# Query units of a hybrid decoder trunk: one copy out of PSUM by ScalarE, all later readers on the copy

## The chip, the core and the metric

The kernel runs on one core of one Trainium2 chip. The metric is device time in microseconds, the median of three runs. Every time below comes from the runs, from the profile of one further execution, or from answers of its trace.

The core's engines are named as follows: PE is TensorE (matmuls; PEld its weight loads), DVE is VectorE, ACT is ScalarE, POOL is GpSimd, SP issues DMAs.

## What is computed

A trunk of two residual layers over 2048 tokens of width 1024, in float32. Each layer normalises its input, projects it, runs three branches with SiLU gates and projects back:

```python
for layer in range(DEPTH):                       # DEPTH = 2
    xn = rms_norm(h, norm_g[layer])
    if layer % 2 == 0:
        u, v, ga, xb, gb, qm, gm = _split(xn @ w_in_even[i], EVEN_SIZES)
        ya = chunked_sgu(u, v, ...) * silu(ga)
        yb = multiscale_pool(xb, b_w[i], b_scale[i]) * silu(gb)
        ym = memory_attention(qm, mem_n, ...) * silu(gm)
    else:
        qc, kc, vc, gc, da, db, gd, qm, gm = _split(xn @ w_in_odd[i], ODD_SIZES)
        yc = swa_sink_attention(qc, kc, vc, ...) * silu(gc)   # 8 heads, window 128
        yd = conformer_conv(da, db, ...) * silu(gd)           # 31 taps
        ym = memory_attention(qm, mem_n, ...) * silu(gm)      # 4 heads, 256 memory rows
    h = h + concatenate([ya_or_yc, yb_or_yd, ym]) @ w_out[i]
```

Both attentions normalise their queries by head (64 wide): `q * rsqrt(mean(q*q) + eps)`.

## The kernel before

**Tiles.** The tokens are cut into four blocks of 512. One block through one layer is a stage; there are four even and four odd stages, run in the order even 0, even 1, odd 0, even 2, odd 1, even 3, odd 2, odd 3. The odd stages begin near 475, 960, 1430 and 1685 us.

**Wide units.** A projection is made in units of 128 output channels by 512 tokens (`proj`): 8 chunks, each three matmuls 128x512 (`mm3`, L126 to L128), since every operand is split into a rounded high half and a low half that holds what the rounding left. So a unit is 24 wide matmuls into one PSUM bank "mm".

**Query units.** `query_steps` makes 32 of them: two memory-query units in each stage, and four window-query units in each odd stage. In a unit, after `proj`:

- `stack_queries` casts each half of the partitions to the high half (ScalarE, L315, 64x512, twice) and subtracts it from the projection to get the low half (VectorE, L123, 64x512, twice). The two halves go to different partitions, so that one score matmul multiplies high and low together.
- ScalarE squares the projection (L363). Four small matmuls (L366, with as many weight loads) sum the squares by head into the bank "pv". VectorE adds a constant (L369, tile qss), GpSimd raises to the power -1/2 (L370).

All five of the first readers read the PSUM bank. The scores (L320, L321) take the query halves as weights and the keys km or kt as moving data.

**PSUM.** Eight banks: two "mm", one "cv", four "tr" (scores and transposes take turns there), one "pv". The sums of squares, the window values (L873), the memory values (L426) and one even-stage product share the one "pv" bank.

**An odd stage.** Its order is a string of steps: f fills (a wide unit of the background list, four query units, gates), S0 to S3 are the window scores of four token tiles, V0 to V3 their values, s0 to s3 and v0 to v3 the same for the memory, g and d the conv's units. The relevant part is "S3 V2 f4 s0 V3 e d2 s1": the fill of four wide units (two memory-query units, then two gates) ahead of s0 and V3. This place is called the tail of the fill phase below; "the last wide unit" is the second gate of that fill.

- A window score step S: 16 score matmuls, copies by ScalarE, masks and maxima by VectorE, eight exponentials with sums by ScalarE (L845), a normalisation by GpSimd (L852).
- A value step V (`swa_values`): eight transposes (L860) into two "tr" banks; of each bank ScalarE copies (L863) and VectorE multiplies by a mask (L864) the four heads' weights, and GpSimd masks ScalarE's copy (L866); eight value matmuls 128x512 (L873); four products by VectorE (L881).
- A gate: one wide unit, tanh by ScalarE (L349), a product by VectorE (L351).
- The depthwise conv is 31 taps on VectorE (L698, 128x512), put between the other VectorE work wherever the scheduler finds room. Memory maxima on VectorE are L407.

**What sets the order.** The source is written in steps; the framework's list scheduler then orders each engine's instructions by a simulated timeline. So the order on every engine is fixed at build time and depends on the durations and dependencies that the scheduler models. An edit in one place can move instructions in others.

Of the kernel before, what the change touches and what calls it, by code (L numbers as in the profile page):

```python
# [12 lines left out]
AF = mybir.ActivationFunctionType  # L13
# [8 lines left out]
TB = 512  # L22
# [30 lines left out]
def trunk(ctx: ExitStack, tc: tile.TileContext, x, mem, par, par1, wkv, w_v, w_cm0, w_kvc, w_cm1, w_o0, w_o1, awt, bw, dpw, abse, out):  # L53
    nc = tc.nc
    V, A, G, T = nc.vector, nc.scalar, nc.gpsimd, nc.tensor
# [26 lines left out]
    def pv_bank():  # L82
        return bank("pv", 1)

    def short(dt=F32):
        return pp_.tile([P, TB + 14], dt, tag="u2", name="u2", bufs=4)

    def half(tag, bufs, dt=F32):
        pool = mov if tag in ("yh", "yl", "q") else sb
        return pool.tile([P, TB], dt, tag=tag, name=tag, bufs=bufs)  # L90

    def small(tag, n):
        return sm.tile([P, n], F32, tag=f"s{n}", name=tag, bufs={1: 6, 2: 6, 4: 8, 6: 2, 8: 10, 16: 4, 32: 2}[n])
# [4 lines left out]
    def par_of(name):  # L98
        t, a, b = _COLS[name]
        return (pc, once)[t][:, a:b]  # L100
# [21 lines left out]
    def lo_of(eng, lo, raw, hi):  # L122
        eng.tensor_tensor(lo, raw, hi.bitcast(F32), op=ALU.subtract)  # L123
# [188 lines left out]
    def stack_queries(pb):  # L312
        qq = [half("q", 8, F32R) for _ in range(2)]
        for g, (rows, other) in enumerate(((lowr, high), (high, lowr))):
            A.copy(qq[g][rows], pb[rows])  # L315
            lo_of(V, qq[g][other], pb[rows], qq[g][rows])
        return qq

    def score(out, q, g, cols, keys):
# [10 lines left out]
    def proj(xn, w_cm, unit, after=None):  # L330
        wh, wl = view(wslot(w_cm[unit], key=("cm", int(w_cm is w_cm1), unit)), "p (k c) -> p k c", k=KC)
        pb = mm_bank()
        for k in range(KC):
            with tc.issue_after(after.ins) if after and k == 0 else ExitStack():
                mm3(pb, wh[:, k, :], wl[:, k, :], xn[0][:, k, :], xn[1][:, k, :], k == 0, k == KC - 1)
        pump(2)
        return pb
# [16 lines left out]
    def query_steps(st, w_cm, units, heads, tag):  # L354
        qs = []
        n_u = len(units)
        r = small(tag, NT * heads).rearrange("p (t h) -> p t h", t=NT)

        def step(n, u):
            pb = proj(st["xn"], w_cm, u)  # L360
            qs.append(stack_queries(pb))
            sq = short()
            A.activation(sq[:, :TB], pb, AF.Square)  # L363
            sp = pv_bank()[:, :2 * NT]
            for tt in range(NT):
                T.matmul(sp[:, 2 * tt:2 * tt + 2], lhsT=sq[:, tt * P:(tt + 1) * P], rhs=par_of("bones"),  # L366
                         start=True, stop=True)
            t = small("qss", 2 * NT)
            V.tensor_scalar(t, sp, 64 * EPS, None, op0=ALU.add)  # L369
            G.tensor_tensor(r[:, :, n:n + n_u + 1:n_u], t.rearrange("p (t g) -> p t g", t=NT),  # L370
                            nhalf[:, :2 * NT].rearrange("p (t g) -> p t g", t=NT), op=ALU.pow)

        return (qs, r), [lambda n=n, u=u: step(n, u) for n, u in enumerate(units)]
# [683 lines left out]
```

## Time and profile before

| | us |
|---|---|
| median of three runs | 1932.83 (1929.33 to 1933.11) |
| profiled execution | 1935.3 |
| its span, first to last instruction | 1933.6 |
| TensorE busy | 1893.0 (98%) |
| VectorE busy | 1113.9 (58%) |
| GpSimd busy | 661.0 (34%) |
| ScalarE busy | 613.7 (32%) |

The span leaves out what lies around the first and the last instruction. Busy time of matmuls is modelled at its end, and matmuls are pipelined, so neighbours overlap in the timeline. In the table of waits a line says which engine, tile and line waited, for whose instruction, how long in all, how often, and the longest time. In a timeline a row is a start, a duration, the engine, the line, the operation, and in brackets the idle time before it and who ended it.

### The profile page before, as it was taken

The page shows a single profiled execution, that of the slowest core. Times are in us where ns is not written, and L with a number is a line of the kernel's source. Part 1 is how long each engine was busy: PE and PEld are TensorE (multiplying, and loading weights), DVE is VectorE, ACT ScalarE, POOL GpSimd, SP SyncE. Part 2 cuts the span into 40 slices and gives each one's busy share as a digit, 9 for nine tenths or more (in the row PEclk, how much of TensorE's full clock was granted, in tenths as well). Part 3 has the DMA queues.
Part 4 walks back from the last instruction along what each step waited for, and adds up shares of the span by engine and source line. Part 5 has one row for each costly group of instructions (what it writes and reads, how often), then busy time and mean ns, then how long its engine had stood idle before and what let it go on. Part 6 is the DMA issues. An engine that isn't in the chain of part 4 may idle for free.

```text
span 1933.6 us, 26042 instructions
## 1 busy us (share of the span) xinstructions
PE 1893.0 (98%) x10034; PEld 1567.7 (81%) x10034; DVE 1113.9 (58%) x2039; ACT 613.7 (32%) x1444; POOL 661.0 (34%) x597
## 2 busy tenths in 40 slices
PE   6999999999999989999999999999999999999999
PEld 6888898888886768888888787988888877888787
DVE  5675423433899552442389955243339985489953
ACT  4454213302354450330223523142021443223412
POOL 4576432514455572340302333133121233302311
PEclk9999999999999999999999999999999999999999
DMA  8688885556876558555664355746575444754334
GB/s 305 219 295 306 284 311 174 200 196 232 316 268 216 209 203 283 183 188 193 240 224 153 130 197 191 245 162 209 177 286 174 137 155 172 261 203 152 130 135 150
DMA packets 72460, 409.00 MB, mean 212 GB/s; under 512 B 7952, under 2 KB 8080, under 8 KB 35344
## 3 DMA queue, kind: packets, MB, share of 16 engines
q1 hardware_dynamic: 72336, 407.33, 60.2%
q8 instruction: 80, 1.31, 0.3%
q14 instruction: 44, 0.36, 0.1%
HBM read 312.67 MB, written 94.63 MB: 211 GB/s over the span
## 4 chain that ended last, share of the span: by engine, by line
PE 87%; DVE 4%; DMA 3%; POOL 3%; ACT 2%; issue 1%; SPq 0%; ACTq 0%; POOLq 0%; DVEq 0%
PE mm L126 21%; PE mm L128 21%; PE mm L127 21%; PE cv L128 4%; PE cv L126 4%; PE cv L127 4%; PE pv L873 2%; PE pv L426 2%; PE tr L320 1%; PE tr L394 1%; POOL w L123 1%; PE tr L321 1%; DVE cv L698 1%; PE pv L366 1%; PE pv L593 1%
## 5 line engine op out<-in xcount | busy, mean ns | idle before, releaser
L126 PE MATMUL mm<-xnh,w 128*128 128x512 f32 x1176 | 463.2, 394 | 1.0 <-ACT u L363 0.9
L128 PE MATMUL mm<-xnh,w 128*128 128x512 f32 x1176 | 459.9, 391 | 0.0
L127 PE MATMUL mm<-xnl,w 128*128 128x512 f32 x1176 | 459.3, 391 | 0.0
L698 DVE SCALAR_TENSOR_TENSOR cv<-hx,dwh,cv 128x512 f32<-128x512 f32 x464 | 349.2, 753 | 9.2
L126 PEld LDWEIGHTS mm<-xnh,w 128*128 128x128 f32 x1176 | 221.1, 188 | 50.2 <-issue 5.6
L128 PEld LDWEIGHTS mm<-xnh,w 128*128 128x128 f32 x1176 | 220.9, 188 | 46.5 <-issue 0.9
L127 PEld LDWEIGHTS mm<-xnl,w 128*128 128x128 f32 x1176 | 221.1, 188 | 43.4 <-issue 0.2
L530 DVE TENSOR_TENSOR row<-mm,row 128x512 f32<-128x512 f32 x160 | 109.8, 690 | 192.9 <-PE mm L128 192.4
L126 PE MATMUL mm<-yh,w 128*128 128x512 f32 x534 | 213.2, 400 | 3.0 <-DVE gt L351 1.6
L127 PE MATMUL mm<-yl,w 128*128 128x512 f32 x534 | 209.2, 392 | 1.5 <-POOL yl L123 1.5
L128 PE MATMUL mm<-yh,w 128*128 128x512 f32 x534 | 209.6, 393 | 0.0
L123 POOL TENSOR_TENSOR w<-wr,w 128x1024 fp32r<-128x1024 f32 x66 | 158.9, 2410 | 121.4 <-ACT w L120 121.3
L123 POOL TENSOR_TENSOR yl<-gt,yh 128x512 fp32r<-128x512 f32 x80 | 102.8, 1298 | 261.0 <-ACT yh L120 261.0
L126 PEld LDWEIGHTS mm<-yh,w 128*128 128x128 f32 x534 | 100.6, 188 | 27.2 <-DVE row L530 3.6
L120 ACT CAST w<-wr 128x1024 fp32r<-128x1024 f32 (+1 forms) x81 | 84.4, 1041 | 113.6 <-DMA wr<-in_w_cm_dram 38.6
L127 PEld LDWEIGHTS mm<-yl,w 128*128 128x128 f32 x534 | 100.7, 189 | 22.0 <-POOL yl L123 1.9
L128 PEld LDWEIGHTS mm<-yh,w 128*128 128x128 f32 x534 | 100.4, 188 | 22.3 <-issue 1.2
L120 ACT CAST yh<-gt 128x512 fp32r<-128x512 f32 x80 | 47.2, 620 | 200.6 <-PE mm L128 76.0
L386 POOL TENSOR_SCALAR p<-p,mrd 128x256 f32<-128x256 f32 x128 | 60.6, 491 | 102.7 <-DVE mrd L415 92.8
L412 ACT ACTIVATE p<-tr,mnb,qm 128x256 f32<-128x256 f32 x128 | 70.6, 561 | 75.6 <-DVE mnb L409 71.5
L126 PE MATMUL mm<-w,xnh 128*128 128x256 f32 x320 | 92.2, 288 | 1.5 <-ACT xnh L120 1.5
L126 PE MATMUL cv<-xnh,w 128*128 128x512 f32 x232 | 92.0, 396 | 0.0
(227 smaller groups left out, 3342.6 us busy)
## 6 DMA issues: line engine op xcount, KB each, us to landing
w<-w_cm SPq DMA_DIRECT2D x132, 1024.0 KB, 4.8
w<-w_o SPq DMA_DIRECT2D x60, 1024.0 KB, 4.9
w_cm<-w SPq DMA_DIRECT2D x44, 1024.0 KB, 4.9
wr<-in_w_cm_dram SPq DMA_DIRECT2D x44, 512.0 KB, 6.2
w_o<-w SPq DMA_DIRECT2D x20, 1024.0 KB, 4.8
w<-w_v SPq DMA_DIRECT2D x12, 1024.0 KB, 7.6
wr<-in_w_o_dram SPq DMA_DIRECT2D x20, 512.0 KB, 5.7
row<-in_x_dram SPq DMA_DIRECT2D x16, 512.0 KB, 5.7
```

What stands on the lines that cost most here:

```text
L120: return A.copy(hi, raw)
L123: eng.tensor_tensor(lo, raw, hi.bitcast(F32), op=ALU.subtract)
L126: T.matmul(out, lhsT=lh, rhs=rh, start=first, stop=False)
L127: T.matmul(out, lhsT=lh, rhs=rl, start=False, stop=False)
L128: T.matmul(out, lhsT=ll, rhs=rh, start=False, stop=last)
L320: T.matmul(out, lhsT=q[g][:, cols], rhs=keys[:, g], start=True, stop=False)
L386: G.tensor_scalar(p[:, h, :], p[:, h, :], rd[:, h:h + 1], 1.0, op0=ALU.mult, op1=ALU.mult)
L412: A.activation(p[:, h, :], banks[h // 2][:, (h % 2) * 256:(h % 2) * 256 + 256], AF.Exp, bias=nb[:, h:h + 1], scale=qr[:, tt, h:h + 1], acc ...
L426: mm = T.matmul(pv[64 * g:64 * g + 64, n * P:(n + 1) * P], lhsT=vm[:, mt, (2 * n + g) * 64:(2 * n + g + 1) * 64], rhs=pt[:, mt, 2 * g + n, :],
L530: add = V.tensor_tensor(row, pb, row, op=ALU.add)
L698: V.scalar_tensor_tensor(dst, src, w, acc, op0=ALU.mult, op1=ALU.add)
L873: mm = T.matmul(pv[64 * g:64 * g + 64, :], lhsT=st["va"][:, tt + m, 64 * g:64 * g + 64], rhs=pts[g][:, m].rearrange("p h t -> p (h t)"), s ...
```

## The change

ScalarE copies each query unit's projection out of PSUM once, into an SBUF tile "qr" (two buffers). The casts, the low halves and the square read this copy. Of the two low halves, the first stays on VectorE, the second goes to GpSimd.

```diff
@@ -313,7 +313,7 @@
         qq = [half("q", 8, F32R) for _ in range(2)]
         for g, (rows, other) in enumerate(((lowr, high), (high, lowr))):
             A.copy(qq[g][rows], pb[rows])
-            lo_of(V, qq[g][other], pb[rows], qq[g][rows])
+            lo_of((V, G)[g], qq[g][other], pb[rows], qq[g][rows])
         return qq
@@ -358,9 +358,11 @@
         def step(n, u):
             pb = proj(st["xn"], w_cm, u)
-            qs.append(stack_queries(pb))
+            raw = half("qr", 2)
+            A.copy(raw, pb)
+            qs.append(stack_queries(raw))
             sq = short()
-            A.activation(sq[:, :TB], pb, AF.Square)
+            A.activation(sq[:, :TB], raw, AF.Square)
```

Lines from the copy (L362) on are two higher in the changed kernel: L363 becomes L365, L366 L368, L369 L371, L407 L409, L698 L700, L845 L847, L860 L862, L863 to L866 become L865 to L868, L873 L875, L881 L883. L349, L351 and the scores L320, L321 keep theirs.

The scheduler's order changes with it. TensorE at the tail of the fill phase in odd stage 2, before: the transposes L860 of the fourth value step and some memory scores stand ahead of the last wide unit (L126 to L128, most of it left out), the first sums of squares L366 in its midst.

```order
L860 MATMUL tr<-ident,p 128x128 x4
L873 MATMUL pv<-pt,va 64x512 x4
L320 MATMUL tr<-km,q 128x256
L321 MATMUL tr<-km,q 128x256
L860 MATMUL tr<-ident,p 128x128 x4
L320 MATMUL tr<-km,q 128x256
L321 MATMUL tr<-km,q 128x256
L126 MATMUL mm<-xnh,w 128x512
...
L366 MATMUL pv<-pc,u_13134 128x2 x4
L128 MATMUL mm<-xnh,w 128x512
L320 MATMUL tr<-km,q 128x256
...
L366 MATMUL pv<-pc,u_13179 128x2 x4
```

Behind the last row come four value matmuls L873 (a row "x4" of L366 or L873 is eight in the trace, where each of these matmuls stands twice). The same place after:

```order
L875 MATMUL pv<-pt,va 64x512 x4
L128 MATMUL mm<-xnh,w 128x512
...
L320 MATMUL tr<-km,q 128x256
L321 MATMUL tr<-km,q 128x256
...
L862 MATMUL tr<-ident,p 128x128 x8
L368 MATMUL pv<-pc,u_13184 128x2 x4
L320 MATMUL tr<-km,q 128x256
...
L368 MATMUL pv<-pc,u_13231 128x2 x4
L875 MATMUL pv<-pt,va 64x512 x4
```

All eight transposes and both sums of squares now stand behind the last wide unit, and between the two sums the eight scores of the second memory tile. The order is of this kind in the three other odd stages too.

VectorE at the same place, before: the evacuations L864 are done between gates and taps of the fill.

```order
L881 SCALAR_TENSOR_TENSOR gt<-pv,gt 128x128 x4
L407 TENSOR_REDUCE mmx<-tr 128x2
L698 SCALAR_TENSOR_TENSOR cv<-hx,dwh,cv 128x512
L351 SCALAR_TENSOR_TENSOR gt<-u_13218,mm 128x512
L407 TENSOR_REDUCE mmx<-tr 128x2
L864 TENSOR_TENSOR pt<-tr,pc 128x512
L698 SCALAR_TENSOR_TENSOR cv<-hx,dwh,cv 128x512 x3
L369 TENSOR_SCALAR qss<-pv 128x8
L698 SCALAR_TENSOR_TENSOR cv<-hx,dwh,cv 128x512
L351 SCALAR_TENSOR_TENSOR gt<-u_13251,mm 128x512
L698 SCALAR_TENSOR_TENSOR cv<-hx,dwh,cv 128x512
L369 TENSOR_SCALAR qss<-pv 128x8
```

After:

```order
L351 SCALAR_TENSOR_TENSOR gt<-u_13270,mm 128x512
L700 SCALAR_TENSOR_TENSOR cv<-hx,dwh,cv 128x512 x6
L883 SCALAR_TENSOR_TENSOR gt<-pv,gt 128x128 x4
L700 SCALAR_TENSOR_TENSOR cv<-hx,dwh,cv 128x512
L409 TENSOR_REDUCE mmx<-tr 128x2 x2
L351 SCALAR_TENSOR_TENSOR gt<-u_13303,mm 128x512
L700 SCALAR_TENSOR_TENSOR cv<-hx,dwh,cv 128x512
L866 TENSOR_TENSOR pt<-tr,pc 128x512 x2
L371 TENSOR_SCALAR qss<-pv 128x8
L700 SCALAR_TENSOR_TENSOR cv<-hx,dwh,cv 128x512 x2
L371 TENSOR_SCALAR qss<-pv 128x8
```

Both evacuations of the transposes (L866) have moved behind the second gate (L351), the maxima (L409) and the fourth products (L883). ScalarE in odd stage 2, after, from the first memory-query unit on: the second unit's copy (L362) stands behind the eight exponentials (L847) of the fourth score step.

```order
L362 COPY qr<-mm 128x512
L315 CAST q<-qr 64x512 x2
L365 ACTIVATE u_13184<-qr 128x512
L847 ACTIVATE p,cde<-p,cnb,qc 128x128 x8
L844 ACTIVATE ces<-ces 128x8
L362 COPY qr<-mm 128x512
L865 COPY pt<-tr 128x512 x2
L315 CAST q<-qr 64x512 x2
L365 ACTIVATE u_13231<-qr 128x512
L349 ACTIVATE u_13270<-mm 128x512
L349 ACTIVATE u_13303<-mm 128x512
L865 COPY pt<-tr 128x512 x2
```

Before, the casts and squares of both units stood in these places, and of the last two copies of transposes (L863) one stood ahead of the second square and one ahead of the last tanh (L349).

## Rows read from the trace of the kernel before

**Rows 1.** The page's first part: busy us, share of the span, instructions of each engine.

```profile
PE 1893.0 (98%) x10034; PEld 1567.7 (81%) x10034; DVE 1113.9 (58%) x2039; ACT 613.7 (32%) x1444; POOL 661.0 (34%) x597
```

**Rows 2.** What TensorE waited for: us in total, times, longest us.

```profile
PE pv L873 <- POOL pt L866: 1.8, 2, 1.5
...
PE tr L320 <- DVE pt L864: 1.5, 3, 1.0
...
PE mm L126 <- ACT u L363: 0.9, 1, 0.9
PE pv L366 <- DVE qss L369: 0.9, 1, 0.9
...
PE pv L873 <- DVE qss L369: 0.6, 1, 0.6
```

**Rows 3.** Casts (ACT's idle time before L315) and low halves (L123; ns min/median/max).

```profile
  DVE q L123: 31.7, 27
...
L123 DVE TENSOR_TENSOR q<-mm,q x56: 683/688/695, 60.7 to 1811.3; 64x512 fp32r<-64x512 f32 x56
```

**Rows 4.** Nearest rows for the added work, by line: ns min/median/max, first and last start.

```profile
L555 ACT COPY hx<-mm x11: 586/587/598, 114.9 to 1285.9; 128x512 f32<-128x512 f32 x11
...
L123 POOL TENSOR_TENSOR yl<-gt,yh x80: 1267/1292/1739, 149.4 to 1909.1; 128x512 fp32r<-128x512 f32 x80
```

**Rows 5.** Timeline of TensorE at the tail in odd stage 2.

```profile
1560.36 0.50 PE L126 MATMUL mm<-xnh,w 128*128 128x512 f32 x1
...
1565.70 0.95 PE L366 MATMUL pv<-pc,u 128*128 128x2 f32 x8
...
1566.83 0.28 PE L320 MATMUL tr<-km,q 128*128 128x256 f32 x1
...
1567.30 0.28 PE L320 MATMUL tr<-km,q 128*128 128x256 f32 x1
...
1569.29 1.94 PE L873 MATMUL pv<-pt,va 128*64 128x512 f32 x8 [0.58 <-DVE qss L369]
```

**Rows 6.** Timeline of VectorE at the same tail.

```profile
1560.45 0.87 DVE L881 SCALAR_TENSOR_TENSOR gt<-pv,gt 128x128 f32<-128x128 f32 x4
...
1561.84 0.75 DVE L698 SCALAR_TENSOR_TENSOR cv<-hx,dwh,cv 128x512 f32<-128x512 f32 x1
1562.49 0.68 DVE L351 SCALAR_TENSOR_TENSOR gt<-u,mm 128x512 f32<-128x512 f32 x1
1563.09 0.68 DVE L407 TENSOR_REDUCE mmx<-tr 128x2 f32<-128x512 f32 x1
1563.69 0.68 DVE L864 TENSOR_TENSOR pt<-tr,pc 128x512 f32<-128x512 f32 x1
1564.29 2.33 DVE L698 SCALAR_TENSOR_TENSOR cv<-hx,dwh,cv 128x512 f32<-128x512 f32 x3
```

**Rows 7.** Timeline of TensorE at the tails of odd stages 0 and 3.

```profile
627.77 3.68 PE L873 MATMUL pv<-pt,va 128*64 128x512 f32 x8 [1.47 <-POOL pt L866]
...
1820.18 0.60 PE L860 MATMUL tr<-ident,p 128*128 128x128 f32 x4
...
1823.74 3.63 PE L873 MATMUL pv<-pt,va 128*64 128x512 f32 x8
```

**Rows 8.** Busy us of PE, PEld, DVE, ACT, POOL, then granted clock, in four stretches.

```profile
627.00:632.00 5.00, 4.23 (x10) 1.29 (x11) 4.82 (x8) 1.91 (x7) 2.33 (x3) 0.50 0.67 210
...
1100.00:1104.00 4.00, 3.68 (x11) 0.89 (x11) 3.89 (x8) 1.44 (x5) 2.10 (x2) 0.57 0.19 76
...
1560.00:1572.00 12.00, 11.31 (x63) 8.62 (x62) 11.59 (x25) 2.33 (x5) 4.43 (x4) 1.00 0.34 124
...
1823.00:1828.00 5.00, 4.92 (x15) 1.91 (x16) 3.64 (x10) 2.55 (x9) 1.64 (x1) 0.66 0.33 136
```

**Rows 9.** VectorE's key low halves (L123, ns min/median/max), and one with GpSimd beside it.

```profile
L123 DVE TENSOR_TENSOR km<-u,km x32: 681/687/2499, 102.6 to 1699.4; 64x512 fp32r<-64x512 f32 x32
...
497.65 2.47 DVE L123 TENSOR_TENSOR km<-u,km 64x512 fp32r<-64x512 f32 x1 [0.53 <-ACT km L308]
...
497.18 2.40 POOL L123 TENSOR_TENSOR w<-wr,w 128x1024 fp32r<-128x1024 f32 x1 [3.52 <-ACT w L120]
```

## The prediction

> **What bounds the kernel now.** I read the page's engine line first: TensorE is busy 1893.0 of 1933.6 us (98%), the other engines a third to three fifths [rows 1]. So an edit that moves work between ScalarE, VectorE and GpSimd is worth only what it does to the 40 us in which TensorE stands still, and to TensorE's clock. The second view is what TensorE waited for [rows 2]. For the bank that the query units hold (L126 behind the Square, L363) it waited once, 0.9 us. For what the odd stages do behind their last wide unit it waited more: 1.8 us for GpSimd's L866, 1.5 us for VectorE's L864, 0.9 and 0.6 us for VectorE's L369, 4.8 us in all. The third is the query unit itself [rows 3]: ScalarE stood 31.7 us behind VectorE's low halves, since both take turns on one bank; ScalarE is not the bound, so that time is free. The fourth is the end of the fill phase in odd stage 2 on TensorE and on VectorE [rows 5, 6], the fifth the same place in other odd stages [rows 7], and the last the granted clock there [rows 8].
>
> What the reader is to see in rows 5 and 6: while TensorE runs the last wide unit (1560.36 to about 1566.8), VectorE empties the transposes of the fourth value block (L864 at 1563.69). When the unit is over, its scores, sums of squares and value matmuls run almost at once; one wait of 0.58 us is left. Where the transposes stand behind the unit, as in odd stage 0, the wait is longer (1.47 us), and the clock is down.
>
> **The change, part by part.**
>
> *The copy.* 32 copies 128x512 by ScalarE. The same engine's copy of that shape takes 0.587 us [rows 4]: 32 x 0.59 = 19 us more on ScalarE, which is busy a third of the span. TensorE sees them only where a copy stands late in ScalarE's queue. In odd stages 0, 2 and 3 the second memory-query copy stands behind eight exponentials; TensorE asks for that bank one wide unit (5.5 us) and the small work beside it (1.3 us) later. I take 0, the bound above is 2 us in all.
>
> *The bank comes free sooner*, after 0.6 us instead of two casts, two low halves and a Square. This can give back only waits that were there: the 0.9 us of rows 2 and about 0.6 us of smaller ones, 1.5 us; none lies below zero.
>
> *Low halves.* VectorE loses 32 x 0.688 = 22 us [rows 3]. GpSimd gains 32 low halves 64x512; its nearest row has twice the partitions, 1.29 us [rows 4]. I take that whole, 41 us; the lower bound is half, 21 us. Neither engine is the bound. The half that waits on GpSimd is wanted by the scores much later: in odd stage 2 the last memory query is ready a whole unit before its scores. So 0, if VectorE's own half is as fast as before (the second rival).
>
> *The moved work* is the term that decides. The order of the rows (the pieces in the section on the change) shows it. Before, in odd stages 1 to 3, some or all of the transposes L860 and part of the memory scores stand ahead of the last wide unit or inside it, and so do their evacuations. After, in all four odd stages, the first sum of squares, all or nearly all transposes (L862), and all eight second-tile scores come behind the last wide unit, then the second sum of squares and the value matmuls (L875). The second-tile scores go into the very banks from which VectorE has to evacuate the transposes (L866), and L875 shares its one bank with both sums of squares, so it waits for VectorE's second L371. Queued ahead of these on VectorE stand the next gate (L351), two maxima (L409), four value products (L883) and conv taps (L700).
>
> Odd stage 2 step by step, T the end of the last wide matmul. Each VectorE instruction counts its duration less the 0.08 us by which neighbours overlap (L351 at 1562.49 lasts 0.68, L407 begins 0.60 later) [rows 6]: gate and maximum and evacuation 0.6, four products 0.8, a tap 0.7, and 0.78 in a row. 23 wide matmuls take 5.34 us [rows 5], a unit so 5.5 us. VectorE can begin the first gate of the tail at T - 4.65 (ScalarE's tanh of 0.6 us lies ahead), and ends it at T - 4.05; six taps to T + 0.6; products 1.4; tap 2.1; two maxima 3.3; gate 3.9; tap 4.6; the two L866 at 5.2 and 5.8; L371 5.9; two taps and L371 at 7.45. TensorE: four scores 0.45 (rows 5: 1566.83 to 1567.30), eight transposes 0.9 (four last 0.60 [rows 7]), the sum of squares 0.9 [rows 5], so it is ready at T + 2.25 and waits until 5.3: **3.05 us**. Four scores, 5.75, wait for the second bank 0.15, four scores and the second sum, 7.25, then 0.3 us for L371. Sum 3.5 us against 0.6 before.
>
> The same steps with each stage's own order give 1.9 us in odd 0, 2.7 in odd 1, and 4.85 in odd 3, where four taps stand ahead of the second L371. Together 13.0 us. Before it was 4.8, so **+8.2 us**. This is worked by hand; one tap more or less ahead in each stage is 0.75 x 4 = 3 us either way.
>
> *The clock.* Around the value matmuls the granted clock is 0.50 in odd 0, 0.57 in odd 1, 0.66 in odd 3, toward the lower level of 1.2 GHz, and 1.00 in odd 2 [rows 8]. In the first and the last of these the eight value matmuls last 3.68 and 3.63 us, in odd 2 1.94 [rows 5, 7]. What went before: in odd 0 seven microseconds with small matmuls and waits, in odd 2 less than three. After, odd 2 has some 7.5 us of the first kind, so I count a fourth fall: **+1.7 us** (3.65 - 1.94). Bounds: -5.1 us, if all three present falls vanish (3 x 1.7), and +5 us, if the longer gaps also slow the wide matmuls that follow.
>
> Sum: +8.2 - 1.5 + 1.7 = +8.4 us. The profiled run took 1935.3 us, its span 1933.6, so the profile of after would be 1943.7; it stands 2.5 us above the median of 1932.83. On the median's base: 1941.2 us.
>
> **The rivals.**
>
> *No change (0.18).* The hand count is pessimistic: VectorE reaches the tails without its six low halves of a stage (6 x 0.69 = 4.1 us less), and where its position rather than a dependency set the wait, each tail costs 2 us. Then 8.0 - 4.8 - 1.5 + 1.7 = +3.4, and with the clock unchanged +1.7: about 1934.5. Against it: the first gate of the tail waits for its unit, so VectorE cannot run ahead of T - 4.65, and the six taps stand behind it.
>
> *VectorE's half is blocked by GpSimd (0.10; slower still).* Before, the low halves read PSUM and the sums lasted 0.683 to 0.695 us in all 56 rows [rows 3]. After, VectorE reads two operands in SBUF. The nearest rows of that kind are km: median 0.687, longest 2.499 [rows 9]; the one at 497.65 took 2.47 us, and GpSimd's w ran from 497.18 to 499.58. The Trainium skill, "SBUF — State Buffer", section "SBUF: two separate sides", has the rule that a VectorE operation with two SBUF inputs and a GpSimd operation hold their common port one at a time, each for its whole instruction; by that rule the change pairs exactly what excludes one another, and the trace agrees with its 2.47 us. In numbers from rows: behind a GpSimd low half a VectorE half loses up to 1.29 us, behind w up to 1.8. One such in front of each tail, at the gate, moves the whole chain by 1.3 to 1.8 us, four times 5 to 7 us: 1946 to 1948. Only where VectorE is on the path does it count, and there one half of a stage stands close.
>
> *Faster (0.12).* The banks are free sooner, the tails wait no longer than now, and no stretch is thin enough for the clock to fall: -1.5 - 5.1 = -6.6, 1926. The price is that of rows 8; it decides if the transposes' evacuation runs as soon as the order lets it on both engines. Against it stands that all of it now lies behind the unit, as in odd 0 before, where the clock fell.
>
> *The change doesn't do what it says* would need ScalarE to wait elsewhere. Its squares and casts no longer wait for VectorE by construction, so I give it no chance of its own.
>
> **How the numbers follow.** The forecast, longer tails, has 0.60, with +4 to +14 us: 1937 to 1947. With the blocked half 0.70 is slower by over 0.2% (3.9 us, about what a measurement of this kernel can tell from no change), 0.18 within it, 0.12 faster. The range holds 8 in 10: from 1930.5, which leaves out the faster case, to 1948.5, which takes in the blocked half's upper price.
>
> **What would show it.** Right: TensorE's waits for L866 (scores L320) rise from 1.5 us to some 7 us and those for L371 to 3 us or more; the value matmuls L875 of the fourth block last 3.4 to 3.7 us in all four odd stages; the wait for the Square is gone; ScalarE about 633 us busy, VectorE about 1092, GpSimd 680 to 702. Wrong: if TensorE's scores at the tails wait under 1 us each, VectorE was earlier than counted; if the value matmuls last 1.9 us in stages where they now last 3.6, the clock term has the other sign; if the low halves q on VectorE have a median well above 0.69 us, the second rival holds.

## The result and the profile after

The changed kernel takes 1947.51 us (median of four runs, 1945.54 to 1948.94) against 1932.97 us before, a ratio of 1.008 (95% interval 1.0066 to 1.0094; a ratio is estimated from all runs, the two medians alone give 1.0075): slower by 14.5 us. 1941.2 us was forecast, with a range of 1930.5 to 1948.5 us. The profiled execution took 1948.33 us, with a span of 1946.6 us, 13.0 us more than the span before.

The engine line of the page after, to be read against [rows 1]:

```profile
PE 1897.8 (97%) x10034; PEld 1571.8 (81%) x10034; DVE 1102.7 (57%) x2007; ACT 636.6 (33%) x1476; POOL 706.4 (36%) x629
```

ScalarE has 22.9 us more, GpSimd 45.4 us more, VectorE only 11.2 us less although 32 low halves of 0.69 us (22 us) left it. TensorE does the same work in 13 us more. What it waited for (us in total, times, longest), to be read against [rows 2]:

```profile
PE tr L320 <- DVE pt L866: 6.4, 5, 2.3
...
PE mm L126 <- DVE gt L351: 4.4, 4, 1.5
PE pv L875 <- DVE qss L371: 3.4, 4, 1.7
PE mm L126 <- ACT qr L362: 2.3, 1, 2.3
...
PE pv L368 <- DVE gt L883: 0.8, 1, 0.8
```

The row for the gates' products (L351) stood so before:

```profile
PE mm L126 <- DVE gt L351: 1.6, 2, 0.8
```

The wait for VectorE's evacuations has grown most (6.4 us against 1.5), then the one for its gates' products (4.4 against 1.6) and the one for its step of the sums of squares (3.4 against 1.5). The wait for the Square is gone, but one of 2.3 us for the copy has come.

**The tail of odd stage 2.** TensorE's timeline after (start, us, line, idle time before it and who ended it), to be read against [rows 5]:

```profile
1568.37 1.04 PE L862 MATMUL tr<-ident,p 128*128 128x128 f32 x8
1569.24 0.95 PE L368 MATMUL pv<-pc,u 128*128 128x2 f32 x8
1572.52 0.58 PE L320 MATMUL tr<-km,q 128*128 128x256 f32 x1 [2.33 <-DVE pt L866]
...
1574.39 1.70 PE L368 MATMUL pv<-pc,u 128*128 128x2 f32 x8
1576.44 3.68 PE L875 MATMUL pv<-pt,va 128*64 128x512 f32 x8 [0.35 <-DVE qss L371]
1580.06 0.79 PE L126 MATMUL mm<-xnh,w 128*128 128x512 f32 x1
1580.65 0.63 PE L127 MATMUL mm<-xnl,w 128*128 128x512 f32 x1
```

VectorE's timeline at the same place, to be read against [rows 6]:

```profile
1561.12 1.50 DVE L123 TENSOR_TENSOR q<-qr,q 64x512 fp32r<-64x512 f32 x1
1562.66 0.69 DVE L351 SCALAR_TENSOR_TENSOR gt<-u,mm 128x512 f32<-128x512 f32 x1
1563.26 4.71 DVE L700 SCALAR_TENSOR_TENSOR cv<-hx,dwh,cv 128x512 f32<-128x512 f32 x6
1567.88 0.88 DVE L883 SCALAR_TENSOR_TENSOR gt<-pv,gt 128x128 f32<-128x128 f32 x4
1568.67 0.75 DVE L700 SCALAR_TENSOR_TENSOR cv<-hx,dwh,cv 128x512 f32<-128x512 f32 x1
1569.33 1.28 DVE L409 TENSOR_REDUCE mmx<-tr 128x2 f32<-128x512 f32 x2
1570.53 0.68 DVE L351 SCALAR_TENSOR_TENSOR gt<-u,mm 128x512 f32<-128x512 f32 x1
1571.12 0.75 DVE L700 SCALAR_TENSOR_TENSOR cv<-hx,dwh,cv 128x512 f32<-128x512 f32 x1
1571.78 1.28 DVE L866 TENSOR_TENSOR pt<-tr,pc 128x512 f32<-128x512 f32 x2
...
1576.13 0.17 DVE L371 TENSOR_SCALAR qss<-pv 128x8 f32<-128x8 f32 x1 [1.53 <-PE pv L368]
```

VectorE has no idle time from 1561.1 to 1573: the evacuations are late because of what stands ahead of them, not because of a dependency of theirs. The transposes were there at 1569.2, the first evacuation begins at 1571.78. TensorE waits 2.33 us for it, and from there on runs at half pace: the eight scores from 1572.52 on take 1.87 us where eight took 0.93 us before, the second sums of squares 1.70 us instead of 0.95, the value matmuls 3.68 us instead of 1.94, and wide matmuls that start 0.43 us apart instead of 0.23. The granted clock of four tails after (columns as in [rows 8]: busy us of five engines, then the clock):

```profile
1569.00:1580.00 11.00, 8.32 (x36) 5.45 (x34) 9.32 (x17) 2.43 (x7) 4.51 (x4) 0.63 0.29 95
1100.00:1110.00 10.00, 7.22 (x31) 4.04 (x31) 9.82 (x21) 2.77 (x10) 4.36 (x4) 0.72 0.01 3
1829.00:1840.00 11.00, 7.75 (x39) 4.51 (x38) 10.79 (x21) 3.03 (x9) 4.51 (x4) 0.76 0.29 97
625.00:635.00 10.00, 8.64 (x34) 5.63 (x34) 8.51 (x19) 2.52 (x6) 5.65 (x4) 0.66 0.93 331
```

All four fall now, odd stage 2 among them.

**Where the 13 us lie.** The first key transposes of the four odd stages start at 481.58, 959.48, 1428.00 and 1681.95 us before, at 481.50, 961.81, 1431.62 and 1691.75 us after. So odd 0 with even 2 costs 2.4 us, odd 1 with even 3 1.3 us, odd 2 6.2 us, odd 3 to the end 3.2 us. Odd 1 costs more than its 1.3 us show: counted from the span's start, the value matmuls there are 4.7 us late, the matmul behind the gate at 1168.9 7.5 us, and then nearly 4 us come back in even 3 (1292.5 us before, 1296.1 after, for the same place), 2.2 of them because it no longer waits for a weight transfer (w_v).

**The copy's wait in odd stage 0.** VectorE's low half at 604.68, with GpSimd's weight split beside it, and what came of it on ScalarE and TensorE:

```profile
604.53 2.39 POOL L123 TENSOR_TENSOR w<-wr,w 128x1024 fp32r<-128x1024 f32 x1
```
```profile
604.68 2.79 DVE L123 TENSOR_TENSOR q<-qr,q 64x512 fp32r<-64x512 f32 x1
```
```profile
609.42 0.50 ACT L847 ACTIVATE p<-p,cnb,qc 128x128 f32<-128x128 f32 x1 [4.66 <-DVE cnb L841]
...
613.82 0.57 ACT L362 COPY qr<-mm 128x512 f32<-128x512 f32 x1
```
```profile
614.45 0.50 PE L126 MATMUL mm<-xnh,w 128*128 128x512 f32 x1 [2.29 <-ACT qr L362]
```

The low half takes 2.79 us instead of 0.69 and ends after GpSimd's w. VectorE's next steps (L840, L841) are late by this, so the eight exponentials on ScalarE begin only at 609.42; the second copy stands behind them, and TensorE, which asked for its bank at 612.16, waits 2.29 us. The kernel before had a holding up at this place too: a step of 128x8 on VectorE (L839, the later L841; median 0.16 us) took 1.70 us beside GpSimd's w, and its exponentials began 0.94 us earlier than those after.

```profile
606.68 1.70 DVE L839 TENSOR_TENSOR cnb<-cnb,nsink 128x8 f32<-128x8 f32 x1
```
```profile
608.48 0.49 ACT L845 ACTIVATE p<-p,cnb,qc 128x128 f32<-128x128 f32 x1 [0.51 <-DVE cnb L839]
```

So 0.9 of the 2.29 us are new lateness; the rest comes of the copy's place behind the eight exponentials (an estimate from these rows).

### The profile page after: what moved, and what is told of

Read it like the earlier page. It is cut to its first block, busy times and chain, and to the rows that moved or that the text cites. A ratio compares the mean times of both kernels' runs of the same rounds, so it can differ in the third digit from the quotient of the medians.

```text
span 1946.6 us, 26114 instructions
## 1 busy us (share of the span) xinstructions
PE 1897.8 (97%) x10034; PEld 1571.8 (81%) x10034; DVE 1102.7 (57%) x2007; ACT 636.6 (33%) x1476; POOL 706.4 (36%) x629
## 4 chain that ended last, share of the span: by engine, by line
PE 78%; DVE 10%; DMA 4%; ACT 3%; POOL 3%; issue 2%; SPq 0%; ACTq 0%; POOLq 0%; DVEq 0%
PE mm L126 19%; PE mm L128 18%; PE mm L127 18%; PE cv L128 4%; DVE cv L700 4%; PE cv L126 4%; PE cv L127 4%; DMA wr<-in_w_cm_dram 2%; POOL w L123 2%; PE pv L428 2%; PE tr L396 1%; PE tr L320 1%; PE tr L321 1%; PE pv L875 1%; PE pv L368 1%
## 5 line engine op out<-in xcount | busy, mean ns | idle before, releaser
L126 PE MATMUL mm<-xnh,w 128*128 128x512 f32 x1176 | 463.6, 394 | 3.6 <-ACT qr L362 2.3
L128 PE MATMUL mm<-xnh,w 128*128 128x512 f32 x1176 | 460.7, 392 | 0.0
L700 DVE SCALAR_TENSOR_TENSOR cv<-hx,dwh,cv 128x512 f32<-128x512 f32 x464 | 349.3, 753 | 9.2
L126 PEld LDWEIGHTS mm<-xnh,w 128*128 128x128 f32 x1176 | 221.6, 188 | 55.2 <-issue 7.1
L128 PEld LDWEIGHTS mm<-xnh,w 128*128 128x128 f32 x1176 | 221.6, 188 | 47.5 <-issue 1.7
L126 PE MATMUL mm<-yh,w 128*128 128x512 f32 x534 | 212.4, 399 | 4.4 <-DVE gt L351 3.1
L128 PE MATMUL mm<-yh,w 128*128 128x512 f32 x534 | 209.8, 393 | 0.0
L123 POOL TENSOR_TENSOR yl<-gt,yh 128x512 fp32r<-128x512 f32 x80 | 102.9, 1299 | 263.8 <-ACT yh L120 263.8
L123 POOL TENSOR_TENSOR w<-wr,w 128x1024 fp32r<-128x1024 f32 x66 | 159.7, 2425 | 95.9 <-ACT w L120 95.8
L126 PEld LDWEIGHTS mm<-yh,w 128*128 128x128 f32 x534 | 100.3, 188 | 28.2 <-DVE gt L351 4.4
L128 PEld LDWEIGHTS mm<-yh,w 128*128 128x128 f32 x534 | 100.2, 188 | 22.4 <-issue 1.4
L123 POOL TENSOR_TENSOR q<-qr,q 64x512 fp32r<-64x512 f32 x32 | 43.8, 1368 | 175.3 <-ACT q L315 170.9
L351 DVE SCALAR_TENSOR_TENSOR gt<-u,mm 128x512 f32<-128x512 f32 x67 | 45.7, 682 | 87.5 <-ACT u L349 87.2
```

The lines of the kernel that those rows point to most:

```text
L126: T.matmul(out, lhsT=lh, rhs=rh, start=first, stop=False)
L128: T.matmul(out, lhsT=ll, rhs=rh, start=False, stop=last)
L351: V.scalar_tensor_tensor(y, th[:, :TB], 1.0, pb, op0=ALU.add, op1=ALU.mult)
L700: V.scalar_tensor_tensor(dst, src, w, acc, op0=ALU.mult, op1=ALU.add)
```

## The experiments

All tails in one table. "Waits" is the time by which matmul starts in the 13 us ahead of the fourth step's value matmuls lie further apart than the same pair of matmuls does in the median; "values" is the time from the first of these eight value matmuls to the next matmul (1.87 at the upper clock). Ratios are to the kernel before, run beside each.

| kernel | waits in odd 0, 1, 2, 3, us | sum | values in odd 0, 1, 2, 3, us | ratio |
|---|---|---|---|---|
| before | 3.1, 0.6, 0.9, 1.0 | 5.6 | 3.6, 3.4, 1.9, 3.6 | 1 |
| after | 3.2, 2.9, 3.2, 3.6 | 12.8 | 3.2, 3.6, 3.6, 3.6 | 1.008 |
| e1 copy only | 4.4, 1.5, 1.2, 3.0 | 10.2 | 3.6, 3.6, 1.9, 3.6 | 1.0054 |
| e2 after, transposes first | 4.1, 0.2, 0.8, 0.8 | 5.9 | 2.4, 1.9, 1.9, 1.9 | 0.9991 |
| e3 before, transposes first | 0.9, 0.8, 0.8, 0.4 | 2.9 | 1.9, 1.9, 1.9, 1.9 | 0.9986 |
| e4 before, transposes last | 3.2, 0.6, 1.1, 1.1 | 5.9 | 3.2, 1.9, 1.9, 3.4 | 1.0001 |
| e5 after, evacuations first | 3.1, 1.5, 1.6, 3.9 | 10.2 | 3.2, 2.9, 3.2, 3.6 | 1.005 |
| e6 after, VectorE's half from PSUM | 3.1, 1.9, 1.5, 1.7 | 8.3 | 3.4, 2.5, 3.2, 3.1 | 1.0039 |
| e7 e6, transposes first | 3.5, 0.0, 0.0, 0.8 | 4.3 | 3.4, 1.9, 1.9, 1.9 | 0.9992 |
| e8 e1, transposes first | 4.2, 0.7, 1.4, 1.5 | 7.8 | 3.6, 1.9, 3.6, 3.0 | 1.0034 |
| e9 before, half the taps | 3.8, 0.0, 1.7, 1.9 | 7.5 | 2.5, 1.9, 1.9, 1.9 | 1.0012 |
| e10 after, half the taps | 3.7, 0.8, 0.8, 0.8 | 6.2 | 3.3, 1.9, 1.9, 1.9 | 0.9998 |
| e11 e3, sums first | 2.5, 0.8, 0.8, 0.4 | 4.4 | 3.5, 1.9, 1.9, 1.9 | 0.9982 |
| e12 e2, sums first | 4.0, 0.2, 0.8, 0.8 | 5.8 | 2.6, 1.9, 1.9, 1.9 | 1.0001 |

The profile's own list of idle times in these tails gives somewhat less, 4.7 us before and 10.9 after. The tail columns are those of the profiled execution, which can lie up to 4 us off the median (e6: 1942.42 against 1938.33).

The ratios follow the two tail columns broadly. About 2 us of each rest on other things that shift with any new order, such as the transfer of w_v and the odd stages' first wait (L725 for VectorE's kn); e12 and e2 have the same tails and differ by 2 us.

**e1: the copy alone.** From the changed kernel, both low halves back on VectorE:

```diff
-            lo_of((V, G)[g], qq[g][other], pb[rows], qq[g][rows])
+            lo_of(V, qq[g][other], pb[rows], qq[g][rows])
```

> The copy alone: both low halves stay on VectorE, reading the copy. Order theory (the time lies at the four tails, where transposes, scores and sums of squares now stand behind the last wide unit): the order of the tails is as in the changed kernel, so TensorE's waits there stay 11 to 15 us in all, the value matmuls of the fourth step last 3.2 to 3.7 us in all four odd stages, and the time is 1942 to 1949 us. GpSimd theory (the time is the price of the low halves that GpSimd does, and of VectorE standing behind them): back to 1931 to 1936 us.

1941.24 us, ratio 1.0054 (1.0038 to 1.007). The order of the tails is of the changed kernel's kind, and two thirds of the loss are there without GpSimd. The rest, some 5 us, comes with the second half being on GpSimd; what of it is GpSimd's work and what the order, which isn't quite the same, these two runs don't tell. The waits were under the 11 us that were expected. So neither theory has all of it.

**e2: the changed kernel, transposes first.** In `swa_values`, around the transposes and the three evacuations:

```diff
+        with tc.high_priority(offset=AHEAD):
             for g in range(2):
                 tb = tr_bank()
                 for n in range(4):
                     T.transpose(...)
                 ...
```

> The whole change, with the transposes of the value steps and their evacuations at high priority in the scheduler, so that in odd stages 1, 2 and 3 they stand inside the last wide unit or ahead of it; in odd stage 0 they still stand behind it. Order theory: the tail waits of odd 1, 2 and 3 fall from about 3 us each to under 1.2 us each and the clock falls for less time or not at all there, while odd 0 keeps its 3 us: 1934 to 1940 us. GpSimd theory: 1944 to 1949 us.

1929.19 us, ratio 0.9991 (0.9981 to 1.0001), 5 us below the expected range, against 1.008 without the priority. With every instruction of the change still there, its whole loss is gone. TensorE, then VectorE, in odd stage 2 of this run:

```profile
1559.21 0.64 PE L863 MATMUL tr<-ident,p 128*128 128x128 f32 x4
...
1562.67 0.28 PE L320 MATMUL tr<-km,q 128*128 128x256 f32 x1
...
1565.87 1.94 PE L876 MATMUL pv<-pt,va 128*64 128x512 f32 x8 [0.75 <-DVE qss L371]
```
```profile
1560.56 0.69 DVE L867 TENSOR_TENSOR pt<-tr,pc 128x512 f32<-128x512 f32 x1 [0.23 <-ACT pt L866]
```

The transposes stand in the midst of the last wide unit, VectorE empties them at once, the value matmuls begin 3.2 us after the unit's end (in the changed kernel 8.5 us, 1567.9 to 1576.44) and run at the upper clock:

```profile
1558.00:1569.00 11.00, 10.25 (x63) 7.95 (x62) 10.66 (x23) 2.64 (x6) 4.46 (x4) 1.00 0.39 144
```

In odd stage 0, where the scheduler left the transposes behind the unit, the wait stayed: VectorE's step L371 stands behind five taps and a gate.

```profile
621.23 3.91 DVE L700 SCALAR_TENSOR_TENSOR cv<-hx,dwh,cv 128x512 f32<-128x512 f32 x5
625.05 0.68 DVE L351 SCALAR_TENSOR_TENSOR gt<-u,mm 128x512 f32<-128x512 f32 x1
625.65 0.75 DVE L700 SCALAR_TENSOR_TENSOR cv<-hx,dwh,cv 128x512 f32<-128x512 f32 x1
626.31 0.16 DVE L371 TENSOR_SCALAR qss<-pv 128x8 f32<-128x8 f32 x1
```
```profile
626.62 1.83 PE L368 MATMUL pv<-pc,u 128*128 128x2 f32 x8 [3.66 <-DVE qss L371]
```

This run also bears on the second rival. Its 32 low halves on VectorE took 29.9 us, as long as in the changed kernel (29.8), and in odd stage 0 one was held up just as there, with the second copy ahead of the exponentials at 606.51:

```profile
602.01 2.80 DVE L123 TENSOR_TENSOR q<-qr,q 64x512 fp32r<-64x512 f32 x1
```

TensorE doesn't wait for the copy here.

**e3: the kernel before, transposes first.** The same edit, on the kernel before.

> The kernel before, with that priority alone: no copy, no low half on GpSimd. The transposes stand ahead of or inside the last wide unit in all four odd stages, odd 0 too. Order theory: the 3 us of waits in odd 0 fall under 1 us and its clock fall with them, the other stages gain little: 1926 to 1931 us, faster than both. GpSimd theory says nothing of it: 1931 to 1935 us.

1929.03 us, ratio 0.9986 (0.9976 to 0.9996). As expected the tail of odd 0 falls from 3.1 to 0.9 us, and all four value groups last 1.87 us. Part of the gain is spent again in odd 0, where a score waits 1.9 us for VectorE's low half, ahead of the 13 us of the table. This is the fair base for e2: with the same priority in both, the change costs 0.2 us by the medians (1929.19 against 1929.03).

**e4: the kernel before, transposes last.** The transposes of the fourth value step are issued behind the last wide matmul:

```diff
+                with tc.issue_after(wide[0].ins) if tt == 3 else ExitStack():
                     T.transpose(tb[:, n * P:(n + 1) * P], pp[:, 4 * g + n, :], ident)
```

> The kernel before, with one order forced: the transposes of the fourth value step are issued behind the last wide unit in every odd stage, as the change does it; first-tile scores stay where the scheduler puts them. No copy, nothing on GpSimd. Order theory: tail waits of 2 to 3.5 us in each of the four odd stages, value matmuls of 3.2 to 3.7 us in all four, 1938 to 1945 us. GpSimd theory: 1931 to 1936 us.

1930.69 us, ratio 1.0001 (0.9992 to 1.0011). The order theory missed this: with all transposes behind the unit in all four stages nothing is lost. VectorE and TensorE in odd stage 2 (lines L353, L867, L322, L876 are the gate, the evacuation, the score and the value matmul here):

```profile
1560.94 0.69 DVE L353 SCALAR_TENSOR_TENSOR gt<-u,mm 128x512 f32<-128x512 f32 x1 [0.21 <-ACT u L351]
1561.54 0.75 DVE L700 SCALAR_TENSOR_TENSOR cv<-hx,dwh,cv 128x512 f32<-128x512 f32 x1
1562.20 1.28 DVE L867 TENSOR_TENSOR pt<-tr,pc 128x512 f32<-128x512 f32 x2
```
```profile
1562.94 0.39 PE L322 MATMUL tr<-km,q 128*128 128x256 f32 x1 [1.06 <-DVE pt L867]
...
1564.20 1.94 PE L876 MATMUL pv<-pt,va 128*64 128x512 f32 x8
```

Here the third step's values and the first memory scores had run earlier, so VectorE had its products and maxima behind it: only a gate and one tap stand between the end of the unit and the evacuations, and the wait is 1.06 us. So it is not by itself where the transposes stand that costs; it may be what VectorE has queued ahead of their evacuation by then. That is the queue theory of the runs that follow; the position theory is its rival.

**e5: the changed kernel, evacuations first.** Only ScalarE's copy and VectorE's product of a value step at high priority, the transposes not:

```diff
+            with tc.high_priority(offset=AHEAD):
                 A.copy(pt[:, 0], tb3)
                 made.append(V.tensor_tensor(pt[:, 1], tb3, ...))
```

> The whole change, with only the two evacuations of a value step's transposes (ScalarE's copy, VectorE's product) at high priority. The eight transposes still stand behind the last wide unit in all four odd stages, but VectorE has four products less ahead of its evacuations there in odd 1, 2 and 3, and the value matmuls of the third step come earlier. Queue theory (the tail's price is what VectorE has queued between the end of the last wide unit and its evacuations): tail waits fall from about 3.2 to 1 to 2 us a stage, 1936 to 1942 us. Position theory (the price is that the transposes stand behind the unit at all): 1943 to 1949 us, as the changed kernel.

1941.07 us, ratio 1.005 (1.0038 to 1.0063). The transposes still stand behind the unit, and the waits in odd 1 and 2 halve (2.9 and 3.2 to 1.5 and 1.6 us). In odd 3, where the four products (L884 here) and two maxima still stood ahead of the evacuations, nothing is gained (3.9 us). Both follow the queue.

**e6: VectorE's half from PSUM.** VectorE's low half reads the bank, GpSimd's the copy:

```diff
-            lo_of((V, G)[g], qq[g][other], pb[rows], qq[g][rows])
+            lo_of((V, G)[g], qq[g][other], (bank, pb)[g][rows], qq[g][rows])
```

> The whole change, but VectorE's own low half reads the PSUM bank instead of the copy, so that it has one operand in SBUF; the casts, the square and GpSimd's half still read the copy. Port theory (VectorE's half is held up by GpSimd because both of its operands lie in SBUF, and this makes the exponentials, the second copy and the first gate of the tails late): all 32 halves last 0.68 to 0.70 us, against 29.9 us in all for 32 in the changed kernel, the 2.3 us wait for the copy in odd stage 0 is gone, and the time is 1936 to 1942 us. If the holding up is harmless: 1944 to 1948 us. The bank is held until VectorE has read it, so the scheduler's order moves too; the waits at the tails tell the two apart.

1938.33 us, ratio 1.0039 (1.0025 to 1.0052). Low halves by line in the changed kernel and in this one (ns min/median/max):

```profile
L123 DVE TENSOR_TENSOR q<-qr,q x32: 684/685/2794, 53.3 to 1820.5; 64x512 fp32r<-64x512 f32 x32
```
```profile
L123 DVE TENSOR_TENSOR q<-mm,q x28: 683/684/686, 63.7 to 1816.6; 64x512 fp32r<-64x512 f32 x28
```

No half is held up, and the wait for the copy is gone. But the bank is released later and the order moved with it (waits 8.3 instead of 12.8 us), so this run alone doesn't say how much of the 8 us gained is the holding up and how much the order. For the mended order, e7 against e2 tells more.

**e7: e6 with transposes first.** Both edits together.

> The kernel of the sixth run with the transposes and their evacuations at high priority: they stand inside or ahead of the last wide unit in all four odd stages, odd 0 too. Queue theory: no tail waits over 1 us for evacuations, clock at its upper level in all four tails: 1924 to 1929 us, faster than the kernel before.

1930.22 us, ratio 0.9992 (0.9983 to 1.0001), not the 1924 to 1929 us expected. Odd 1 to 3 wait 0.8 us together; odd 0 keeps 3.5 us and its slow value matmuls, and the first wait of an odd stage is 3.0 us instead of 1.4. The transposes of odd 0 stand ahead of the unit as expected (at 614.39), yet VectorE's evacuations come only at 624.91 and 627.57, behind the third step's value matmuls (622.05), and two waits of 1.20 and 1.06 us are left: position alone doesn't save them. Against e2 (ratio 0.9991) this kernel differs in that none of its 32 low halves is held up (21.9 us instead of 29.9), and it is no faster, though its order differs too.

**e8: e1 with transposes first.** Against e2 only the second low half is elsewhere.

> The copy, both low halves on VectorE from the copy, transposes and evacuations at high priority; odd 0 keeps its transposes behind the last wide unit, the other three have them inside it. Against the second run this differs only in where the second low half is done. If GpSimd's halves cost by themselves, it is 2 to 5 us faster than the second run (1924 to 1927 us); if they cost only through the tails' order, within 2 us of it (1927 to 1931 us).

1937.96 us, ratio 1.0034 (1.0022 to 1.0046): some 8 us slower than e2 (0.9991), where it was expected to be faster or the same. In this pair of orders the halves on GpSimd do not cost, they help: without them VectorE is busy 15 us longer (1117.2 against 1102.4), and TensorE's waits in odd 2 and 3 are 1.4 and 1.5 us instead of 0.8, with slow value matmuls in both. The rest of the order differs too, so that the longer queue is the reason is argued, not shown.

**e9 and e10: half the taps.** Both kernels with every second tap of the convolution:

```diff
-        bg.extend(lambda k=k: tap(k) for k in range(TAPS))
+        bg.extend(lambda k=k: tap(k) for k in range(0, TAPS, 2))
```

> The kernel before with only every second tap of the depthwise convolution (16 of 31; the output leaves out the others), so that VectorE has some 170 us less to do. It is the base for the next run. Queue theory: tail waits under 1 us a stage; 1920 to 1930 us. Position theory: its tails as in the kernel before, 1929 to 1933 us.

> The whole change with only every second tap (16 of 31; the output leaves out the others). All memory scores, all transposes of the fourth step and one sum of squares still stand behind the last wide unit in all four odd stages. Queue theory (the price is VectorE's backlog of taps, maxima, gates and products ahead of its evacuations): tail waits under 1.5 us a stage, within 4 us of the run before it. Position theory (the price is that this work stands behind the unit): 10 us or more above the run before it.

1932.45 us (ratio 1.0012, 1.0003 to 1.0021) and 1930.02 us (0.9998, 0.9989 to 1.0007). The change that costs 14.5 us with all taps is 2.4 us faster with half of them. The order in e10 is the changed kernel's kind: all memory scores and transposes behind the last wide unit in all four stages. VectorE and TensorE in odd stage 2 of e10:

```profile
1560.72 0.69 DVE L351 SCALAR_TENSOR_TENSOR gt<-u,mm 128x512 f32<-128x512 f32 x1 [2.19 <-ACT u L349]
1561.32 1.28 DVE L409 TENSOR_REDUCE mmx<-tr 128x2 f32<-128x512 f32 x2
1562.52 0.68 DVE L866 TENSOR_TENSOR pt<-tr,pc 128x512 f32<-128x512 f32 x1
```
```profile
1563.26 0.39 PE L320 MATMUL tr<-km,q 128*128 128x256 f32 x1 [0.56 <-DVE pt L866]
```

VectorE waits for the last gate (2.19 us idle) instead of being behind, and TensorE waits 0.56 us instead of 2.33. This decides for the queue theory and against the position theory in odd 1 to 3. In odd 0 the 3.7 us stay, against the expectation; there VectorE itself stands idle 1.29 us for ScalarE's copy L865, so this wait isn't VectorE's queue. e9 missed the 1920 to 1930 us and the waits under 1 us that the queue theory expected of it: its transposes moved behind the unit in odd 0, 2 and 3, and the waits there grew.

**e11 and e12: the sums' step first.** e3 and e2 with VectorE's small addition to the sums of squares at high priority too.

```diff
+            with tc.high_priority(offset=AHEAD):
                 V.tensor_scalar(t, sp, 64 * EPS, None, op0=ALU.add)
```

> The third run (the kernel before, transposes and evacuations first) with VectorE's small step of the sums of squares at high priority too. Queue theory: its remaining waits for that step (1.9 us) shrink; 1926 to 1930 us, faster than the kernel before by 1 to 4 us. Otherwise as the third run.

> The second run (the whole change, transposes and evacuations first) with VectorE's small step of the sums of squares at high priority too. Queue theory: the wait of 3.7 us for that step in odd stage 0, which stands behind five taps and a gate, shrinks to under 2 us; 1925 to 1929 us.

e11: 1927.67 us, ratio 0.9982 (0.9974 to 0.9991), the fastest of all, faster than both kernels. It is e3's gain, and the runs don't tell the two apart; odd 0's value matmuls are slow again. e12: 1931.25 us, ratio 1.0001 (0.9992 to 1.001); the step in odd 0 still waits 3.6 us, so the edit did not do what it was to do. Between e11 and e12, which have this priority in both kernels, the change still costs 3.6 us, where between e3 and e2 it cost 0.2 and between e9 and e10 it gained 2.4: once the tails are mended, what is left of it differs with the order by some 3 us either way.

## Why the prediction was right, and where not

**The mechanism was right.** TensorE's waits behind the last wide unit, with the clock that falls by them, carry the loss: without them in odd 1 to 3 (e2), with all of the change in place, the time is that of the kernel before. The measured 1947.51 us is just above the 1937 to 1947 us of the forecast's own case and lies in the 1946 to 1948 us of the second rival, so the time alone wouldn't have told the two apart; e2 and e7 do. The range held it by 1 us, at its upper end.

**The moved work** was put at 13.0 us of waits after against 4.8 before; by the table they are 12.8 against 5.6, +7.2 us where +8.2 was taken. By stage the hand count gave 1.9, 2.7, 3.5 and 4.85 us; measured were 3.2, 2.9, 3.2 and 3.6. That the sums agree so well is in part luck: odd 0 was 1.3 us too low and odd 3 1.25 us too high. By the profile's list of waits, from which the 4.8 us were read, the four tails after have 2.2, 2.8, 2.7 and 3.3 us, so +6.2 us from 4.7 to 10.9. The step that T, gate, taps, products, maxima, gate, tap, evacuation follow each other without a gap is what VectorE's timeline shows; in odd 2 it began 0.6 us earlier than counted, and the first wait is 2.33 us instead of 3.05.

**The clock term was sized too small;** it is the term of the sum that failed. +1.7 us was taken, from one more slow group of value matmuls. That group is there, and the four groups together grew by just that (12.4 to 14.1 us). More has come on top: behind the value matmuls the first wide matmuls run at half pace, which costs some 1.0 us more in each of odd 1, 2 and 3 by the distances of their starts (0.5 us less in odd 0), and the small matmuls ahead of the values do so too, in odd 2 for 1.7 us (eight scores 1.87 us instead of 0.93, the second sums of squares 1.70 instead of 0.95) and in odd 0 for some 1.3 us more than before. This is some 5.5 us, with the value matmuls some 7, beyond the bound of +5 us, and it is most of what the forecast lacked of the 14.5 us.

**The copy** was taken at 0 with a bound of 2 us; it cost 2.29 us in odd 0, beyond the bound. The step that failed is that ScalarE would be through its eight exponentials when TensorE asks for the bank (612.16): they began at 609.42, behind VectorE's held-up low half and 0.9 us later than before, and the copy behind them at 613.82. In e2, where the copy stands ahead of them, the same holding up costs TensorE nothing.

**The relief** was put at 1.5 us; 1.2 can be seen (0.9 us for the Square and 0.3 us of a score for VectorE's low half are gone), and 2.8 us came elsewhere: a gate's product on VectorE made TensorE wait 1.33 us at 568.0 and 1.46 us at 1168.9, neither of which the prediction had. Even 3's wait for w_v, 2.2 us, is gone, where everything comes 7 us later than before: a gain that nobody planned.

**The second rival came true in part.** VectorE's 32 halves took 29.8 us instead of 21.9, 7.9 us held up. Thirteen were longer than 0.72 us, and when each of these began, and when no other did, a GpSimd instruction was under way. Three were the halves in front of the tails' first gates (1.5 us instead of 0.69 at 1091.0, 1561.1 and 1820.5), where the rival had put them, but at 0.8 us each and not 1.3 to 1.8, and one is the 2.79 us at 604.68. By the prediction's own sign, a median well above 0.69 us, the rival doesn't hold: the median is 0.685. The rule of the Trainium skill, "SBUF — State Buffer", section "SBUF: two separate sides", on the port that VectorE and GpSimd share agrees with these rows, and with e6, where one operand in PSUM takes all of it away. By itself it costs nothing that can be measured: e2 has as much of it and e7 has none, at the same time (ratios 0.9991 and 0.9992, with orders that are not quite the same). In the changed order, where it stands in front of late tails, how many of the 14.5 us are due to it no run separates: e1 still has it, e6 moved the order.

**The signs** that the prediction named came but for two: the value matmuls last 3.68 us in odd 1 to 3, but 3.29 in odd 0, and GpSimd's 706.4 us lie above 680 to 702. VectorE's 1102.7 us against the 1092 expected is for the most part the 7.9 us held up.

**The faster case** needed evacuations that keep up with the order; VectorE's rows show that they do not. **The no-change case** needed VectorE ahead of its place; its rows show no idle time in 12 us.

**Why the order moved at all** was read from the two programs, and e1 bears it out: with the copy alone the transposes and scores go behind the unit. With the bank free after 0.6 us, the scheduler always has a wide unit ready for TensorE; before, the wait for the bank made the gaps in which it put transposes and scores. That a wait of the simulated timeline was what filled the queue in a good order is argued from this, not shown by a run of its own.

## What to carry to other kernels

An edit that frees a resource sooner also changes what a list scheduler finds ready; read the new order at the places where the bound engine has least slack, and count there what the helper engine has queued between the last long matmul and the evacuation that is waited for. If the loss is there, first try a priority on the small matmuls and evacuations that feed the next dependency: it gave back the whole loss here, and 1.6 to 3.0 us (e3 and e11, ratios 0.9986 and 0.9982) to the kernel before. It is no cure for every order: the copy alone kept 0.34% of its 0.54% with it (e8 against e1). When a wait lengthens on TensorE, price the clock over all that runs after it until the clock is back, not only over the next group.

## What the runs showed of the hardware

After the waits of 2 to 4 us in the tails the granted clock goes toward the lower level of 1.2 GHz, and the cost is longer than the waits: in odd stage 2 matmuls ran at half pace from the end of the 2.33 us wait at 1572.5 to beyond 1581.9, over 9 us. In e4's odd 2, with a wait of 1.06 us in the same place (granted clock 1.00 from 1557 to 1568), the value matmuls took 1.94 us and the clock held; in the kernel before it fell in odd 1 after waits of 0.6 us [rows 8]. So the wait alone doesn't tell whether it falls.

Reading the copy from SBUF made ScalarE's casts and Square a little slower, not faster: 0.62 and 0.63 us against 0.58 and 0.60 from PSUM. GpSimd's subtraction of 64x512 took 1.29 us, just as that of 128x512 [rows 4]: half the partitions are no cheaper there.

A VectorE subtraction 64x512 with both operands in SBUF took 0.685 us where GpSimd was idle at its start, and 0.78 to 2.79 us in all 13 of 32 cases where GpSimd had an instruction under way; with one operand in PSUM (e6) all 32 took 0.683 to 0.686 us.
